# Weight sums in buffers of their own, output gates at eviction, a gate row folded into the output weights, four FFN tiles begun early

## The chip, the cores and the metric

The kernel runs on one core of a Trainium2 chip, as one launch. The time is that of the device in microseconds (us). Each kernel is timed several times and the median counts; one further execution is recorded by the hardware profiler.

## The reference

One block of a hybrid network on x of 1024 tokens by 1024 features, in float32. Cut to what matters here:

```
shift1, scale1, gate1, shift2, scale2, gate2 = split(silu(c) @ w_ada + b_ada, 6)
h = rms_norm(x) * (1 + scale1) + shift1
z, xbc, dt, qk, v, o, if_pre, gate_pre = split(h @ w_in)
y_ssd   = ssd_branch(z, xbc, dt, ...)                        # 2048 wide
y_mlstm = sigmoid(o) * (rms_norm(mlstm(qk, v, if_pre)) * norm_w)   # 4 heads of 512
g_ssd, g_mlstm = split(sigmoid(gate_pre), 2)
merged = g_ssd * (y_ssd @ w_branch_ssd) + g_mlstm * (y_mlstm @ w_branch_mlstm)
x = x + gate1 * (merged @ w_out)
h2 = rms_norm(x) * (1 + scale2) + shift2
gt, up = split(h2 @ w_ffn_in, 2)                             # 2816 wide each
x = x + gate2 * ((silu(gt) * up) @ w_ffn_out)
out = rms_norm(x) * final_norm_w
```

## The kernel before

Every float32 product is made as three matmuls of float32r operands: each operand is split into a rounded part and a rest (a cast on ScalarE, ACT, and a subtraction on VectorE, DVE; the helpers `split`, L123, and `split_pair`, L786), and high by high, high by low and low by high are summed in PSUM. TensorE (PE) thus works through some 12300 matmuls, most of them 128x128 by 128x512.

The program has these stages, in the order of the trace. First the modulation and the normalised, transposed x. Then the SSD branch: `conv_tile`, `z_gate` and `gate_tile` each call `gemm`, 48 matmuls against one 512 KB tile of `w_in`, and `ssd_pair` does the scan. Then the mLSTM, four heads: `ml_q`, `ml_k`, `ml_v` and `ml_scan`, with the gate tiles that are left set between the heads (`GP`, `GZ`). Then four projections by `strassen` (`ssd`, `ml`, `out`, and at the end `ffn`): each halves both operands in both directions and makes seven products instead of eight (p1 to p7), over sums and differences of quarters. Before `ffn` stands the FFN loop, 22 steps of the same kind over `w_ffn_in`: `head(j)` (24 matmuls, needs only the first half of the tokens) and five products (60 matmuls).

The weight side of `strassen` is prepared ahead by `prep_steps` and written to DRAM (`fac_*`): for each block of 128 rows all seven quarters and sums, A11, A12, A22, S1 to S4, split into two parts. `ssd`, `ml` and `out` are prepared between the tiles of the mLSTM stage; their raw rows take the ring `ld` and the split parts `fh`, `fl` the ring `cr`, both shared with the SSD scan and with `conv_tile`. `ffn` is prepared in the FFN loop, in the rings `raw`, `wh` and `wl` that also carry the weights of `head`. The writes go through the queue of GpSimd (POOL), nearly all loads through that of SyncE (SP).

`token_tile` loads 128x1024 tokens at the first use of a block; for `ml` it also loads the o gates into `og` (one buffer) and multiplies (L905, L906). The outputs of `out` are multiplied by gate1 (`g1`) after the product; scratch tiles `c`, `xr`, `sq`, `t2` share one ring of four buffers.

Nobody writes the order of the instructions on an engine by hand: a scheduler takes each instruction as early as its operands, buffers and engine allow, so that the size of a ring decides how early work can begin.

Of the kernel before, what the change touches and what calls it, by code (L numbers as in the profile page):

```python
# [15 lines left out]
P = 128  # L16
# [19 lines left out]
def hybrid_layer(ctx: ExitStack, tc: tile.TileContext, a: dict, out: bass.AP, dbg=None):  # L36
# [106 lines left out]
    FA = {"A11": 0, "A12": 1, "A22": 2, "S2": 3, "S3": 4, "S4": 5, "S1": 6}  # L143
    fac_d = {n: tc.dram_tile([kk, 7, P, 2, 512], F32, name=f"fac_{n}") for n, kk in (("ssd", 8), ("ml", 8), ("out", 4), ("ffn", 11))}

    def prep_steps(name, w_d, rawf, pairf):
        fd = fac_d[name]
        n = fd.shape[0]

        def put(r, kk, p0, cnt):  # L150
            wh, wl = pairf()
            m = cnt * 512
            A.copy(wh[:, 0:m], r[:, 0:m])  # L153
            V.tensor_tensor(wl[:, 0:m], r[:, 0:m], f(wh[:, 0:m]), SUB)  # L154
            for t, w in enumerate((wh, wl)):
                G.dma_start(fd[kk, p0:p0 + cnt, :, t, :].rearrange("f p n -> p f n"), f(w[:, 0:m]).rearrange("p (f n) -> p f n", n=512))

        for kk in range(n):
            r0, r1 = rawf(), rawf()
            Q.dma_start(r0, w_d[kk * P:(kk + 1) * P, :])  # L160
            Q.dma_start(r1, w_d[(kk + n) * P:(kk + n + 1) * P, :])
            put(r0, kk, FA["A11"], 1)
            yield
            put(r1, kk, FA["A12"], 2)
            a11, a21, a12, a22 = r0[:, 0:512], r0[:, 512:], r1[:, 0:512], r1[:, 512:]
            V.tensor_tensor(a22, a21, a22, ADD)
# [146 lines left out]
    def gemm(src, epi, w=None):  # L313
# [10 lines left out]
        next(later, None)  # L324

# [20 lines left out]
    def gate_tile(j):  # L346
# [7 lines left out]
        for _ in range(2):  # L354
            next(preps, None)
# [191 lines left out]
    def z_gate(r, Y=None):  # L547
# [14 lines left out]
        for _ in range(2):  # L562
            next(preps, None)
# [16 lines left out]
    def ml_v(h):  # L580

        vt = [xf("vt") for _ in range(4)]
        for u in range(2):
# [6 lines left out]
            for i in range(4):  # L590
# [14 lines left out]
                else:  # L605
# [9 lines left out]
    def ml_scan(h, q, k, v):  # L615
        C = ap.tile([P, 2, 514], F32, name="C")
        CH = CL = None
        for c in range(NCH):
# [79 lines left out]
            A.copy(yb[:, :, (c % 2) * L:(c % 2 + 1) * L], hps.rearrange("p (j l) -> p j l", l=L))  # L698
# [3 lines left out]
    gates = list(range(32))  # L702
# [16 lines left out]
    def phase_a_pair():  # L719
        return [ap.tile([P, 1024], F32R, name=n, tag="cr", bufs=NCR) for n in ("fh", "fl")]  # L720

    preps = chain(*(prep_steps(n, w, lambda: ld("fr"), phase_a_pair) for n, w in
                    (("ssd", a["w_branch_ssd"][0]), ("ml", a["w_branch_mlstm"][0]), ("out", a["w_out"][0]))))
# [67 lines left out]
    def strassen(name, b0, b1, order, sink, wq, nw, tq, nt, tmp, rows=False, odd=0):  # L791


        fd = fac_d[name]
        n = fd.shape[0]
        B0, B1 = {}, {}

        def t0(k):
            if k not in B0:
                B0[k] = b0(k)  # L800
            return B0[k]

        def t1(k):
            if k not in B1:
                B1[k] = b1(k)
            return B1[k]

        def tok(p, k):
            if p == 6:
                t2 = tmp()  # L810
                V.tensor_tensor(t2, t1(k)[:, H_], t0(k)[:, L_], SUB)
                m = split_pair(t2, tq, "tf", "tf", nt)
                V.tensor_tensor(t1(k)[:, L_], t1(k)[:, L_], t2, SUB)
                return m
            src = {1: lambda: t0(k)[:, L_], 2: lambda: t1(k)[:, L_], 3: lambda: t1(k)[:, H_], 4: lambda: t1(k)[:, L_],
                   5: lambda: t0(k)[:, L_], 7: lambda: t0(k)[:, H_]}[p]()
            m = split_pair(src, tq, "tf", "tf", nt)
            if p == 2:
# [31 lines left out]
    def sink_of(ut, tmp, final):  # L850

        U, U3 = {}, {}

        def sink(p, i, bank):
# [3 lines left out]
            elif p == 2:  # L858
                c = tmp()
                V.tensor_tensor(c, bank, U[i], ADD)  # L860
                final(0, 0, i, c)
# [24 lines left out]
    pb1, pb0 = pool(ctxD, "b1"), pool(ctxD, "b0")  # L886
# [364 lines left out]
```

## Time and profile before

| | |
|---|---|
| three runs | 2781.64, 2789.95, 2791.85 us; median 2789.95 |
| profiled execution | 2794.04 us, span of the trace 2792.3 us |
| PE busy | 2557.2 us (92%), mean granted clock 0.96 |
| DVE, ACT, POOL busy | 1795.5, 1105.2, 558.3 us |
| moved by DMA | 528.86 MB, mean 189 GB/s |

PE is busy nearly all the time, so the places where it is not are what to look for. A busy PE is not always at its full pace: the number of matmuls in a stretch tells more than the busy time.

### The profile page before, as it was taken

To read this page: it belongs to the slowest core of one execution; us is meant where nothing else is said; L and a number is where in the kernel's file an instruction comes from. 1 tells how busy PE (TensorE), PEld (TensorE's weight loads), DVE (VectorE), ACT (ScalarE), POOL (GpSimd) and SP (SyncE) were. 2 spreads that over 40 slices of the span, in tenths; PEclk is the share of its full clock that TensorE was granted. 3 is DMA by queue.
4 is the path that set the end of the run, shared out by engine and by line. 5 is a ranking of instruction groups with operands and counts; after the bars stand their busy time and mean duration, and the time that the engine had idled before them with its cause. 6 is when DMAs were issued, how large, how long until landed. Compare 5 with 4: busy or idle time off the path is not lost.

```text
span 2792.3 us, 34946 instructions
## 1 busy us (share of the span) xinstructions
PE 2557.2 (92%) x12907; PEld 2125.6 (76%) x12907; DVE 1795.5 (64%) x2768; ACT 1105.2 (40%) x1923; POOL 558.3 (20%) x627
## 2 busy tenths in 40 slices
PE   6999989999998999999999999797778999997898
PEld 4788878889876887988988778586557777775686
DVE  7577766895854566456555357554786878885436
ACT  5445544554442344345444423222253333332222
POOL 4000021110432013113133000000134444450001
PEclk9999999999999999999999999898889999998899
DMA  6333332345688458527654769565545666668566
GB/s 193 101 91 114 96 110 85 118 149 159 207 292 282 153 178 265 190 82 264 199 167 151 273 225 394 179 213 190 172 145 162 194 221 215 212 224 318 165 194 236
DMA packets 327826, 528.86 MB, mean 189 GB/s; under 512 B 21952, under 2 KB 208672, under 8 KB 327656
## 3 DMA queue, kind: packets, MB, share of 16 engines
q1 hardware_dynamic: 284968, 376.13, 42.7%
q0 software_dynamic: 42688, 150.49, 14.4%
q8 instruction: 102, 1.67, 0.2%
q14 instruction: 68, 0.56, 0.1%
HBM read 354.28 MB, written 172.27 MB: 189 GB/s over the span
## 4 chain that ended last, share of the span: by engine, by line
PE 59%; DMA 13%; DVE 12%; issue 8%; POOL 4%; ACT 3%; SPq 0%; POOLq 0%; DVEq 0%; ACTq 0%
PE mm L321 25%; PE n L838 10%; PE mm L601 7%; PE mm L838 5%; PE sc L838 4%; PE n L655 2%; DVE sw L786 1%; DMA raw<-in_w_ffn_out_dram 1%; DVE wl L154 1%; DMA fac_ffn<-wl 1%; DMA raw<-in_w_ffn_in_dram 1%; PE n L530 1%; DMA xr<-in_x_dram 1%; PE n L673 1%; PE n L1046 1%
## 5 line engine op out<-in xcount | busy, mean ns | idle before, releaser
L321 PE MATMUL mm<-hh,wh 128*128 128x512 f32 x1392 | 555.5, 399 | 31.9 <-ACT xf L333 20.7
L321 PE MATMUL mm<-hl,wh 128*128 128x512 f32 x1392 | 553.0, 397 | 0.0
L321 PE MATMUL mm<-hh,wl 128*128 128x512 f32 x1392 | 553.0, 397 | 0.0
L321 PEld LDWEIGHTS mm<-hh,wh 128*128 128x128 f32 x1392 | 265.1, 190 | 85.9 <-ACT xf L333 21.6
L321 PEld LDWEIGHTS mm<-hh,wl 128*128 128x128 f32 x1392 | 264.9, 190 | 52.9 <-issue 0.5
L321 PEld LDWEIGHTS mm<-hl,wh 128*128 128x128 f32 x1392 | 265.2, 191 | 51.7 <-issue 0.2
L123 DVE TENSOR_TENSOR wl<-raw,wh 128x1024 fp32r<-128x1024 f32 x126 | 158.6, 1259 | 153.2 <-PE mm L321 69.2
L122 ACT CAST wh<-raw 128x1024 fp32r<-128x1024 f32 x126 | 131.7, 1045 | 217.8 <-DMA raw<-in_w_in_dram 69.3
L786 DVE TENSOR_TENSOR tf<-bt,tf 128x512 fp32r<-128x512 f32 x162 | 110.6, 690 | 159.9 <-ACT tf L785 159.9
L785 ACT CAST tf<-bt 128x512 fp32r<-128x512 f32 x162 | 99.8, 621 | 255.0 <-PE sc L838 130.1
L154 DVE TENSOR_TENSOR fl<-fr,fh 128x512 fp32r<-128x512 f32 (+1 forms) x80 | 88.2, 1102 | 133.7 <-DMA fac_ssd<-fl 46.1
L341 DVE SCALAR_TENSOR_TENSOR xf<-cr,pk,xf 128x1023 f32<-128x1023 f32 (+2 forms) x120 | 160.2, 1336 | 17.8 <-ACT xf L333 16.7
L1046 PE MATMUL n<-t,sw 128*128 128x512 f32 x552 | 145.6, 409 | 25.9 <-ACT sw L785 7.7
L838 PE MATMUL n<-tf,wf 128*128 128x512 f32 x672 | 157.8, 393 | 9.7 <-ACT tf L785 7.8
L838 PEld LDWEIGHTS n<-tf,wf 128*128 128x128 f32 x672 | 127.3, 190 | 37.7 <-ACT tf L785 8.2
L838 PE MATMUL n<-wf,tf 128*128 128x512 f32 x540 | 129.5, 398 | 23.8 <-ACT tf L785 16.9
L1046 PEld LDWEIGHTS n<-t,sw 128*128 128x128 f32 x552 | 106.5, 196 | 56.0 <-ACT t L785 9.5
L838 PEld LDWEIGHTS n<-wf,tf 128*128 128x128 f32 x540 | 103.7, 193 | 47.0 <-ACT tf L785 17.4
L838 PE MATMUL mm<-wf,tf 128*128 128x512 f32 x360 | 97.9, 404 | 26.0 <-ACT tf L785 16.0
L153 ACT CAST fh<-fr 128x512 fp32r<-128x512 f32 (+1 forms) x80 | 75.4, 942 | 115.3 <-DMA fac_ml<-fh 28.8
L503 ACT ACTIVATE ab<-ab,gsum 128x128 f32<-128x128 f32 x256 | 78.4, 389 | 83.0 <-DMA ab<-acs_d 77.8
L559 POOL TENSOR_TENSOR Y<-Y,tz 128x512 f32<-128x512 f32 x14 | 31.0, 2236 | 389.0 <-DVE Y L540 222.5
(436 smaller groups left out, 5160.1 us busy)
## 6 DMA issues: line engine op xcount, KB each, us to landing
raw<-in_w_in_dram SPq DMA_DIRECT2D x104, 512.0 KB, 4.6
wf<-fac_ffn SPq DMA_DIRECT2D x77, 512.0 KB, 4.4
wf<-fac_ssd SPq DMA_DIRECT2D x56, 512.0 KB, 4.9
wf<-fac_ml SPq DMA_DIRECT2D x56, 512.0 KB, 3.7
rw<-in_w_ffn_in_dram SPq DMA_DIRECT2D x42, 512.0 KB, 4.5
raw<-in_w_ada_dram SPq DMA_DIRECT2D x40, 512.0 KB, 4.7
fac_ffn<-wh POOLq DMA_DIRECT2D x33, 512.0 KB, 4.2
fac_ffn<-wl POOLq DMA_DIRECT2D x33, 512.0 KB, 6.1
```

Of the source, the lines that this page charges most:

```text
L122: A.copy(wh, raw)
L123: V.tensor_tensor(wl, raw, f(wh), SUB)
L153: A.copy(wh[:, 0:m], r[:, 0:m])
L154: V.tensor_tensor(wl[:, 0:m], r[:, 0:m], f(wh[:, 0:m]), SUB)
L321: T.matmul(ps, lhsT=ww[:, k, :], rhs=xx[:, halves(hf)], start=n == 0, stop=n == 23)
L341: V.scalar_tensor_tensor(dst[:, sh:], cr[:, :S - sh], cw[:, 3 - sh, ti:ti + 1], dst[:, sh:], MUL, ADD)
L503: A.activation(ab[q][:, e, c], ab[q][:, e, c], AF.Relu, scale=-1.0, bias=acs_t[:, 4 * q + c, h0 + e:h0 + e + 1])
L601: T.matmul(ps[:, c], lhsT=hT[k][x_][:, sl], rhs=ws[k // 4][w_][:, k % 4], start=n == 0, stop=n == 23)
L785: A.copy(m[:, 0], t)
L786: V.tensor_tensor(m[:, 1], t, f(m[:, 0]), SUB)
L838: T.matmul(bk[i], lhsT=st[:, x, sl], rhs=mv[:, y], start=k == 0 and m == 0, stop=k == n - 1 and m == 2)
L1046: T.matmul(bank, lhsT=ww[:, k, :], rhs=b[k][:, r_], start=k == 0 and n == 0, stop=k == 3 and n == 2)
```

## The change

There are five parts. (1) `prep_steps` has buffers of its own: `pr` (two, for raw rows) and `pf` (one, for both split parts, written by one DMA). For `ssd`, `ml` and `ffn` it makes only S1 to S4; A11, A12 and A22 are loaded raw in `strassen` (`wt`) and split at use. `ffn` is prepared in the same chain, and none in the FFN loop; two steps follow each `gemm` and each part of `ml_v`. (2) The o gates are the first gate tiles (`ORD_G`), and `ml_scan` multiplies by them where it evicts its transposed output. (3) gate1 multiplies the rows of `w_out` in `prep_steps`, so the products of `out` need no multiplication. (4) Token blocks are loaded and scaled by half tiles of 128x512, and the scratch tiles have rings of their own. (5) Four heads of the FFN are begun ahead in place of two. The space for descriptors of GpSimd's DMAs is set to 2048 bytes a partition.

```diff
-    FA = {"A11": 0, "A12": 1, "A22": 2, "S2": 3, "S3": 4, "S4": 5, "S1": 6}
+    FA = {"S2": 0, "S3": 1, "S4": 2, "S1": 3, "A11": 4, "A12": 5, "A22": 6}
...
+        def pf():
+            return ap.tile([P, 2, 512], F32R, name="pf", bufs=1)
+
+        def put(r, kk, fa):
+            m = pf()
+            A.copy(m[:, 0], r)
+            V.tensor_tensor(m[:, 1], r, f(m[:, 0]), SUB)
+            G.dma_start(fd[kk, FA[fa]], f(m))
...
-            r0, r1 = rawf(), rawf()
+            r0, r1 = (ap.tile([P, 1024], F32, name="pr", bufs=2) for _ in range(2))
...
+            if gate is not None:
+                g = f(pf()).rearrange("p two n -> p (two n)")
+                Q.dma_start(g, gr_d[gate:gate + 1, :].broadcast_to([P, D]))
+                for r in (r0, r1):
+                    V.tensor_tensor(r, r, g, MUL)
+                yield
...
-            A.copy(yb[:, :, (c % 2) * L:(c % 2 + 1) * L], hps.rearrange("p (j l) -> p j l", l=L))
+            og = ap.tile([P, 4, L], F32, name="og", bufs=1)
+            Q.dma_start(og, tg_d[(16 + 4 * h) * P:(20 + 4 * h) * P, sl].rearrange("(j p) l -> p j l", p=P))
+            V.scalar_tensor_tensor(yb[:, :, (c % 2) * L:(c % 2 + 1) * L], og, 1.0, hps.rearrange("p (j l) -> p j l", l=L), ADD, MUL)
...
+    preps = chain(prep_steps("ssd"), prep_steps("ml"), prep_steps("out", 0), prep_steps("ffn"))
...
+        def weight(fa, k):
+            if FA[fa] < fd.shape[1]:
+                w = wq.tile([P, 2, 512], F32R, name="wf", tag="wf", bufs=nw)
+                Q.dma_start(f(w), fd[k, FA[fa]])
+                return w
+            t = wt_()
+            r0 = (k if fa == "A11" else k + n) * P
+            Q.dma_start(t, w_d[r0:r0 + P, halves(fa == "A22")])
+            return split_pair(t, wq, "wf", "wf", nw)
...
-        if g0 is not None:
-            og = sg.tile([P, 1024], F32, name="og", tag="og", bufs=1)
-            Q.dma_start(og, tg_d[(g0 + k) * P:(g0 + k + 1) * P, :])
-            V.scalar_tensor_tensor(t, og, 1.0, t, ADD, MUL)
...
+            Q.dma_start(t[:, halves(j)], src[r // 4][(r % 4) * P:(r % 4 + 1) * P, halves(j)])
+            A.activation(t[:, halves(j)], t[:, halves(j)], AF.Copy, scale=nw[:, r:r + 1])
...
+    def x_rows(tj, i, ci):
+        return rows_in(po, x_in, 4 * tj + i, ci, 6)
...
-    heads = [head(0), head(1)]
+    heads = [head(j) for j in range(NHEAD)]
...
-        if j % 2 == 0:
-            for _ in range(4):
-                next(preps, None)
```

On ACT, in the second group of the SSD scan, stood before:

```order
L332 COPY cr<-mm 128x512
L333 ACTIVATE xf<-mm,pk_108 128x512
L504 ACTIVATE ab<-ab 128x1024
L539 COPY Y<-n_1171 128x128
L503 ACTIVATE ab<-ab,gsum 128x128 x8
L332 COPY cr<-mm 128x512
L333 ACTIVATE xf<-mm,pk_108 128x512
L504 ACTIVATE ab<-ab 128x1024
L342 ACTIVATE cr<-xf 128x1024
```

and at the same place now (L158 is the cast of a weight sum, L345 the eviction of a convolution tile):

```order
L344 COPY cr<-mm 128x512
L345 ACTIVATE xf<-mm,pk_108 128x512
L513 ACTIVATE ab<-ab,gsum 128x128 x8
L514 ACTIVATE ab<-ab 128x1024
L158 CAST pf<-pr 128x512
L549 COPY Y<-n_1171 128x128
L513 ACTIVATE ab<-ab,gsum 128x128 x8
L344 COPY cr<-mm 128x512
L345 ACTIVATE xf<-mm,pk_108 128x512
L514 ACTIVATE ab<-ab 128x1024
L354 ACTIVATE cr<-xf 128x1024
L158 CAST pf<-pr 128x512
```

The casts of `pf` stand in the SSD stage, where no preparation was. Counting the evictions of convolution tiles (the first two come from another bank, the rest as `xf<-mm`), the 64 of `ssd` and `ml` have all come by the 48th; the 72 of `out` and `ffn` follow between the 56th eviction and the end of the third head's v, which comes after the 72nd.

On DVE, in the middle of the FFN loop, one step held before (L154, L166 to L169: preparation of `ffn`; L786: sums of `w_ffn_in`; the rest evicts products):

```order
L786 TENSOR_TENSOR sw<-s_18858,sw 128x512
L154 TENSOR_TENSOR wl<-raw,wh 128x1024
L1146 TENSOR_TENSOR u_18649<-mm,u_18649 128x512
L786 TENSOR_TENSOR sw<-rw,sw 128x512
L166 TENSOR_TENSOR raw<-raw 128x512
L1149 SCALAR_TENSOR_TENSOR u_18649<-tg,u_18649 128x512
L167 TENSOR_TENSOR raw<-raw 128x512
L1150 SCALAR_TENSOR_TENSOR u_18649<-u_18649,up 128x512
L168 TENSOR_TENSOR raw<-raw 128x512
L169 TENSOR_TENSOR raw<-raw 128x512
```

and the same step holds now (L125: split of a head's weights; L793: sums of `w_ffn_in`):

```order
L1126 TENSOR_TENSOR u_18629<-mm,u_18629 128x512
L793 TENSOR_TENSOR sw<-rw,sw 128x512
L1129 TENSOR_TENSOR u_19127<-sc,u_18629 128x512
L793 TENSOR_TENSOR sw<-rw,sw 128x512
L1132 TENSOR_TENSOR up<-n_19129,u_19127 128x512
L1133 TENSOR_TENSOR u_18629<-n_19129,u_18629 128x512
L793 TENSOR_TENSOR sw<-s_19089,sw 128x512
L1062 TENSOR_TENSOR v<-n_19055,u_19053 128x512
L125 TENSOR_TENSOR wl<-raw,wh 128x1024
```

The five instructions of the preparation are gone from it.

On SP's queue, in the middle of the `ssd` projection, the blocks of the `ml` projection are now loaded while the sums of `ssd` still stream in:

```order
L915 DMA bt<-y_d_79 128x512 x2
L813 DMA wf<-fac_ssd 128x1024
L915 DMA bt<-y_d_79 128x512 x2
L813 DMA wf<-fac_ssd 128x1024
L915 DMA bt<-y_d_79 128x512 x2
```

where before the loads of the o gates stood apart, each behind the last one's buffer, up into the loads of `fac_ml`:

```order
L905 DMA og<-tg_d 128x1024
L830 DMA wf<-fac_ml 128x1024 x2
L897 DMA tgl<-tg_d 128x512
L830 DMA wf<-fac_ml 128x1024
L905 DMA og<-tg_d 128x1024
L830 DMA wf<-fac_ml 128x1024 x2
```

The `og` loads have left this stage; the 32 of `ml_scan` are smaller and stand in the mLSTM stage.

## Rows read from the trace of the kernel before

**Rows 1.** Engines by stretch: busy us (instructions) of each, PE clock, DMA share, GB/s

```profile
0.00:100.00 100.00, 67.80 (x268) 47.71 (x269) 71.47 (x115) 52.96 (x115) 33.39 (x32) 0.93 0.55 161
100.00:640.00 540.00, 526.96 (x3062) 439.68 (x3061) 399.41 (x593) 274.10 (x546) 57.00 (x34) 0.99 0.35 111
740.00:920.00 180.00, 154.00 (x726) 128.84 (x726) 102.48 (x164) 66.48 (x102) 53.81 (x77) 0.91 0.79 268
1560.00:1620.00 60.00, 49.98 (x208) 39.41 (x207) 32.92 (x52) 22.15 (x32) 0.54 (x1) 0.96 0.79 276
1760.00:1800.00 40.00, 24.26 (x77) 17.55 (x78) 27.36 (x42) 10.02 (x14) 0.00 (x0) 0.79 0.48 162
1920.00:1960.00 40.00, 21.40 (x82) 16.71 (x81) 16.93 (x27) 8.93 (x19) 0.00 (x0) 0.74 0.43 140
2000.00:2120.00 120.00, 75.56 (x272) 55.26 (x271) 91.13 (x124) 55.30 (x96) 46.68 (x46) 0.76 0.43 137
2120.00:2500.00 380.00, 362.01 (x1546) 290.29 (x1545) 306.88 (x382) 132.23 (x200) 173.00 (x183) 0.99 0.66 213
2500.00:2580.00 80.00, 58.88 (x224) 46.32 (x223) 49.17 (x70) 16.36 (x26) 11.84 (x14) 0.83 0.81 304
2600.00:2640.00 40.00, 26.83 (x101) 20.58 (x100) 23.33 (x38) 8.28 (x17) 0.00 (x0) 0.79 0.44 135
2640.00:2760.00 120.00, 120.00 (x531) 99.38 (x530) 61.98 (x96) 31.12 (x56) 2.31 (x4) 1.00 0.69 221
```

**Rows 2.** Waits from 700 to 930 us: us in total, times, longest

```profile
PE mm L321 <- ACT xf L333: 16.4, 1, 16.4
...
ACT cr L332 <- DMA fac_ssd<-fh: 5.1, 1, 5.1
```

**Rows 3.** Chain that ended last, from 1740 to 1800 us: start, us, what

```profile
1753.56 4.45 DMA og<-tg_d
...
1758.03 1.24 DVE bt L906
```

**Rows 4.** Chain that ended last, from 1900 to 2125 us

```profile
1932.91 6.63 DMA xr<-in_x_dram
...
1984.63 4.78 DMA xr<-in_x_dram
...
2075.84 5.49 DMA fac_ffn<-wl
```

**Rows 5.** Chain that ended last, from 2120 to 2500 us

```profile
2191.61 10.32 DMA raw<-in_w_ffn_in_dram
```

**Rows 6.** Chain that ended last, from 2480 to 2660 us

```profile
2535.48 12.35 DMA bt<-act_d
```

**Rows 7.** Evictions of convolution tiles up to 560 and 640 us: ns, first and last start

```profile
L333 ACT ACTIVATE xf<-mm,pk x46: 769/783/799, 92.5 to 557.4; 128x512 f32<-128x512 f32 x46
L333 ACT ACTIVATE xf<-mm,pk x54: 769/783/799, 92.5 to 619.6; 128x512 f32<-128x512 f32 x54
```

**Rows 8.** ACT in order of time, first and eighth eviction of the third head's v

```profile
1163.50 0.59 ACT L602 COPY vt<-mm 128x512 f32<-128x512 f32 x1 [4.08 <-PE mm L601]
...
1204.14 0.59 ACT L602 COPY vt<-mm 128x512 f32<-128x512 f32 x1
```

**Rows 9.** Groups by line and shape: busy us, mean ns, idle before

```profile
L154 DVE TENSOR_TENSOR wl<-raw,wh 128x1024 fp32r<-128x1024 f32 x33 | 52.1, 1579 | 6.7 <-DMA fac_ffn<-wl 6.3 <-ACT wh L153 0.4
...
L154 DVE TENSOR_TENSOR fl<-fr,fh 128x512 fp32r<-128x512 f32 x20 | 14.2, 711 | 27.6 <-DMA fac_ssd<-fl 16.2 <-DMA fac_ml<-fl 9.1 <-DMA fac_out<-fl 0.9
...
L166 DVE TENSOR_TENSOR fr<-fr 128x512 f32<-128x512 f32 x20 | 13.7, 686 | 0.2
...
L153 ACT CAST fh<-fr 128x512 fp32r<-128x512 f32 x20 | 12.4, 622 | 31.2 <-DMA fac_ssd<-fh 12.2 <-DVE fl L154 6.6 <-DMA fac_ml<-fh 4.3
```

**Rows 10.** DMA issues by line: count, KB each, median us to landing

```profile
fac_ml<-fh POOLq DMA_DIRECT2D x24, 512.0 KB, 4.3
...
xr<-in_x_dram SPq DMA_DIRECT2D x16, 256.0 KB, 4.1
```

More of the change, by code (lines that the diff above doesn't have):

```diff
@@ L165, in prep_steps @@
             a11, a21, a12, a22 = r0[:, 0:512], r0[:, 512:], r1[:, 0:512], r1[:, 512:]
+            if fd.shape[1] == 7:
+                for fa, x in (("A11", a11), ("A12", a12), ("A22", a22)):
+                    put(x, kk, fa)
+                    yield
             V.tensor_tensor(a22, a21, a22, ADD)
@@ L324, in gemm @@
         next(later, None)
+        for _ in range(2):
+            next(preps, None)
     def conv_tile(col, cw, cb, ti, pre=None):
@@ L561, in z_gate @@
         gemm(w_in[:, OFF_Z + r * P:OFF_Z + (r + 1) * P], epi)
-        for _ in range(2):
-            next(preps, None)
         Q.dma_start(dst, Y)
@@ L604, in ml_v @@
                     next(later, None)
-                else:
+                for _ in range(2):
                     next(preps, None)
@@ L717, in hybrid_layer @@
     later = chain(mod_steps(2, mod_row, 0), mod_steps(3, mod_cols, 2), mod_steps(4, mod_cols, 3), mod_steps(5, mod_row, 1))
[L719 to L723, printed above, removed]
+    gp(2)
+    preps = chain(prep_steps("ssd"), prep_steps("ml"), prep_steps("out", 0), prep_steps("ffn"))
     q, k, v = ml_q(0), ml_k(0), ml_v(0)
@@ L789, in hybrid_layer, with strassen, blk @@
     L_, H_ = halves(0), halves(1)
-    def strassen(name, b0, b1, order, sink, wq, nw, tq, nt, tmp, rows=False, odd=0):
-        fd = fac_d[name]
+    def strassen(name, load, order, sink, wq, nw, tq, nt, wt_, t2_, rows=False, odd=0):
+        fd, w_d = fac_d[name], w_of[name]
         n = fd.shape[0]
[L796 to L806, printed above, removed]
+        B = {}
+        def blk(k, i, j):
+            if (k, i, j) not in B:
+                B[k, i, j] = load(k, i, j)[:, halves(j)]
+            return B[k, i, j]
+        def weight(fa, k):
[7 more added lines that the diff above has]
+            return split_pair(t, wq, "wf", "wf", nw)
@@ L1114, in rw_tile @@
         return e1[0].tile([P, 1024], F32, name="rw", tag="rw", bufs=3)
-    preps = prep_steps("ffn", a["w_ffn_out"][0], raw_tile, lambda: [wp.tile([P, 1024], F32R, name=n, bufs=b) for n, b in (("wh", NWH), ("wl", NWL))])
     for j in range(NFF):
@@ L1151, in hybrid_layer @@
                 G.dma_start(act_d[j * P:(j + 1) * P, H_], u1)
-        if j + 2 < NFF:
-            heads.append(head(j + 2))
-        if j % 2 == 0:
-            for _ in range(4):
-                next(preps, None)
+        if j + NHEAD < NFF:
+            heads.append(head(j + NHEAD))
     ctxF.close()
```

258 lines of the change are left out of this document (115 added, 143 removed).

## The prediction

> **What bounds the kernel now.** I read the table of engines by stretch first, because PE's 92% hides where it loses time. Where PE is undisturbed, 531 matmuls take 120 us, 0.226 us each; a stretch's length less its matmuls at that price is what PE loses there. The reader is to see in [rows 1] that the loss sits in a few places: 60 − 208 × 0.226 = 13.0 us at the start of the projections, 22.6 between `ssd` and `ml`, 21.5 inside `out`, 58.5 between `out` and the FFN loop (its 64 transposes are priced as full matmuls, so this is a lower bound), 30.6 over the FFN loop, 29.4 at the start of the last projection and 17.2 at its second turn. Together 193 us. The front half is nearly full: 527 of 540 us busy in the SSD stage, 26 us idle from 740 to 920. The chain of waits then says what PE waits for in each place, and the groups by shape give prices.
>
> **The FFN loop.** Preparing `ffn` leaves it. Its 33 wide subtractions alone took 52.1 us of DVE [rows 9], and with 11 narrow ones and 44 sums of at least 0.686 about 90 us, of DVE's 307 in 380 [rows 1]. The loop's waits follow from shared rings and an engine in order: a head's weights waited up to 10.32 us [rows 5]. Without it DVE falls to about 220 in 380 and `raw` serves the heads alone. POOL's own sums (173 us of 380) and the chains inside a step stay, so I don't take all 30.6: it falls to about 10, **−20**. Bounds: −8, if POOL's chains cause most of it, and −28.
>
> **Between `out` and the loop.** In the trace, loads of x rows stand in the chain at 1984.63, since their ring is shared with three kinds of scratch, and a write of `fac_ffn` holds it 5.49 us at 2075.84 [rows 4]. Both go: x rows have six buffers, g1's multiplications are gone, the preparation too. Two more heads, 48 matmuls or 10.8 us of PE work, can fill the gap, but they need 512 KB of weights each and two more DVE splits, where DVE is busy 91 of 120 us. The x1 write, which the in-place scaling still waits for, remains. From 58.5 to about 38, **−20** (−8 to −35).
>
> **The turns of the projections.** At 1753.56 the chain shows an `og` load of 4.45 us and its multiplication, 1.24 [rows 3]; one buffer, so four of these run in series while PE needs 12 × 0.226 = 2.7 us per block. That disappears, and the order of SP now has the `ml` blocks loaded during `ssd`. What comes in its place on ACT is per block of p1 one half-tile scaling and two casts, about 3 × 0.622 = 1.9 us [rows 9], and of p2 two and two, 2.5 us of PE's 2.7. That is close, so I leave 5 of 22.6. Inside `out`, p2's evictions wait for x rows, 6.63 us the first [rows 4]; with six buffers they come early: 21.5 to 6. At the start, p1 needs a 256 KB half and a 256 KB weight per block in place of 512 and 512: 13 to 6. Sum −17.6 − 15.5 − 7 = **−40** (−20 to −50).
>
> **The last projection.** Its blocks took 12.35 us at 2535.48 [rows 6], with DMA busy 0.81 [rows 1]: all token rows were loaded whole for p1. Half of those bytes now belong to p2, and p1's weights are half as many. The old h0 tiles come free two steps earlier. At the turn from p2 to p6 the x1 rows no longer share a ring. Of 29.4 + 17.2 I keep 21: **−25** (−10 to −36).
>
> Halving has its other side. A 256 KB load lands in 4.1 us, a 512 KB write in 4.3 [rows 10], so a half costs nearly the latency of a whole. [...] It becomes the third rival below.
>
> **The front half pays.** The order puts casts of `pf` into the SSD stage, not only into the mLSTM. There DVE is at 399 of 540 us; 64 subtractions at 0.711 and 64 sums at 0.686 [rows 9] are 89 us, some 78 of them after the first 100 us: 477 of 540, 88%. PE waits there for PSUM evictions by ACT, which has room (274 plus 64 × 0.622 = 40). I take 6 us (0 to 30). In the first 100 us DVE has 71, and is the engine that the start waits for; the order has there about 8 subtractions and 8 sums, 11 us, and two megabytes of loads ahead of modulation weights: 7 us (0 to 15). Together **+13**.
>
> **The mLSTM stage.** Before, PE lost 16.4 us at one eviction, because ACT waited for a `cr` buffer that a write of `fac_ssd` still read [rows 2]. That tie is gone. But each put now has one buffer: cast 0.622, subtraction 0.711, issue, and landing 4.3 [rows 10], about 6.4 with 0.7 for POOL's issue taken as the subtraction's size. The 64 of `ssd` and `ml` have up to 557 us, 8.5 each from 15 on; the 72 of `out` and `ffn` from 620 [rows 7] to about 1205, the last of eight evictions of the third head's v [rows 8], 8.1 each. So the chain keeps up on average. Beside those evictions of v the order has one put each, and they come (1204.14 − 1163.50) / 7 = 5.8 us apart [rows 8]: there ACT waits about 0.6 us each time, and two puts bunch elsewhere. Loading the o gates adds one 256 KB load per chunk, needed only at its end, and moves 32 evictions from ACT to DVE; nothing is queued behind them but the next chunk. Of the 26 us I take back **−12** (−26 to +15).
>
> [...]
>
> **The sum.** −20 − 20 − 40 − 25 + 13 − 12 = −104. From the profiled execution's 2794 that is **2690 us**. The runs' median stands 4 us below the profiled execution, which is within their spread, so I don't shift it. In the same way 0.5% (14 us) is about what a measurement can tell from no change.
>
> **The rivals.** *First, the one buffer paces everything* (the other side). If a put took c us, the chain needs 64c by the end of the SSD stage and 72c in the mLSTM. SP and ACT are in order: raw rows that wait for `pr`, and casts that wait for `pf`, hold back weight loads and evictions behind them, so PE falls behind with the chain. The lag is 64(c − 8.5) + 72(c − 8.1). The other terms give −92, so it breaks even at c = (92 + 544 + 583)/136 = 9.0 and is slower by 14 us at 9.1. At c = 8.6 it costs 6 + 36 = 42 and gives 2794 − 92 + 42 = 2744. For it speaks that an ACT at half load and a DVE at 88% delay each step, and that a smaller descriptor space might make POOL's issues wait; against it, that 8.1 is 27% above 6.4. Chance 0.10 for around 2744, 0.04 beyond 2808.
>
> *Second, DVE becomes the bound of the SSD stage.* If half of the 78 us shows, the +6 become +39: 2723. Against it, PE's evictions there are ACT's. Chance 0.10.
>
> *Third, the halves gain nothing at the starts*: 4.1 against 4.3 us [rows 10]. Then the first start and the last projection's first 80 us keep their loss: +7 and, of the 25, about 16 back: 2713. Chance 0.12.
>
> *Fourth, all goes its way*: every term at its better bound, −28 − 35 − 50 − 36 − 26 + 0 = −175, 2619; half-way between, about 2655. Chance 0.12.
>
> *Fifth, the waits only move*: PE's losses in FFN and `out` come back as waits on ACT and POOL; every gain at its lesser bound, −8 − 8 − 20 − 10 + 15 + 13 = −18: 2776. Chance 0.08.
>
> **How the numbers follow.** My forecast, 2690 with its own range 2660 to 2720, has 0.44. The second and third lie just above it, the first at 2744, the fourth below. 2645 to 2755 leaves out the slow end of the first, the fifth and half of the fourth's lower part: about 0.18. Faster by 14 us or more: all but the slow end and half of the fifth (2776 lies near the bound), 0.92; same 0.04; slower 0.04.
>
> **What would show it.** In the trace after: no `og`, `bt` or `xr` load of several us in the chain between 1550 and 2000; in the FFN loop some 90 matmuls per 20 us; DVE near 88% in the SSD stage with PE still above 95%; POOL's waits on the cast and the subtraction of `pf` short, and a spacing of about 8 us between its casts. I am wrong if casts of `pf` come at the pace of their DMA with PE idle beside them, if PE waits for DVE in the SSD stage, or if the FFN loop keeps its waits without the preparation.

## The result and the profile after

The changed kernel takes 2698.22 us (median of four runs, 2696.39 to 2699.43), the kernel before 2789.51 beside it: a ratio of 0.9677, with a 95% interval of 0.9657 to 0.9697. The forecast was 2690, with a range of 2645 to 2755. The profiled execution has a span of 2696.5 us.

The table of engines by stretch, of the changed kernel, in the columns of [rows 1]:

```profile
0.00:100.00 100.00, 63.20 (x251) 43.34 (x251) 74.35 (x119) 53.46 (x117) 36.47 (x38) 0.97 0.70 214
100.00:640.00 540.00, 498.08 (x2733) 409.24 (x2734) 433.94 (x645) 281.13 (x564) 82.84 (x91) 0.96 0.58 184
...
1590.00:1650.00 60.00, 58.71 (x260) 48.27 (x259) 47.67 (x77) 36.21 (x65) 1.08 (x2) 1.00 0.64 207
1790.00:1830.00 40.00, 35.34 (x143) 28.22 (x142) 26.70 (x44) 7.96 (x13) 0.00 (x0) 0.91 0.56 177
...
2000.00:2080.00 80.00, 60.30 (x229) 45.79 (x228) 62.31 (x86) 43.58 (x75) 25.38 (x21) 0.80 0.38 116
2080.00:2440.00 360.00, 360.00 (x1575) 295.76 (x1575) 232.49 (x313) 102.07 (x162) 127.49 (x117) 1.00 0.34 103
2440.00:2520.00 80.00, 65.53 (x281) 53.61 (x280) 57.54 (x91) 31.38 (x55) 3.76 (x6) 0.91 0.73 263
```

The back half is now nearly full: 1575 matmuls in the 360 us of the FFN loop are 0.229 us each. The front half is not. From 100 to 640 us PE is busy 498 us where it was 527 [rows 1]: 28.9 us more of idle, at a lower granted clock (0.96 against 0.99), with DVE busier. So the front has to be read as closely as the back, although the total is close to the forecast. The groups of the convolution, gate and q/k matmuls by line (count, ns, first and last start) date the end of the front half, before and after:

```profile
L321 PE MATMUL mm<-hh,wl x1392: 387/389/632, 76.3 to 1560.3; 128*128 128x512 f32 x199
```

```profile
L331 PE MATMUL mm<-hh,wl x1392: 387/389/796, 84.1 to 1597.3; 128*128 128x512 f32 x199
```

The last of them starts 37 us later than before. The kernel loses 37 us up to there and wins 133 after it.

To compare stages whose work has moved, I price every matmul of a trace by the spacing that its shape has where PE runs undisturbed: 0.226 us for 512 columns, 0.120 for 256, 0.119 for 258, 0.109 for 128 (0.058 with 64 stationary columns). What a stage lasts beyond the prices of the matmuls that start in it is PE's loss there. The boundaries are: 100 and 640 us; the last matmul of the rows above; the last of the third projection; the last of the FFN loop's first step; the last of the loop; the end. All in us:

| stage | before | after | change | forecast |
|---|---|---|---|---|
| startup, 0 to 100 | 52.0 | 55.9 | +3.9 | +7 |
| SSD, 100 to 640 | 36.7 | 80.6 | +43.9 | +6 |
| mLSTM, to 1560.3 and 1597.3 | 56.1 | 45.3 | −10.8 | −12 |
| first three projections, to 2000.8 and 1990.2 | 60.7 | 13.2 | −47.5 | −40 |
| gap to the FFN loop, to 2101.4 and 2075.3 | 63.6 | 37.3 | −26.3 | −20 |
| FFN loop, to 2529.2 and 2458.8 | 40.2 | 6.7 | −33.5 | −20 |
| last projection, to the end | 54.1 | 28.6 | −25.5 | −25 |
| sum | 363.4 | 267.5 | −95.8 | −104 |

The sum is the difference of the two spans. The total came out 8 us from the forecast because two errors nearly cancel: the first three rows are 36 us worse than forecast, the other four 28 us better.

The waits of PE from 100 to 640 us in the changed kernel (us in total, times, longest) show whom it waits for now:

```profile
PE mm L331 <- ACT xf L345: 7.1, 4, 4.8
PE sc L485 <- DVE xf L355: 5.2, 2, 5.1
...
PE n L527 <- DVE xe L524: 3.1, 1, 3.1
...
PE n L544 <- DVE st L534: 2.4, 2, 1.6
```

No single wait carries the loss. All the waits that the view lists add up to 43 us, in 21 waits; before the change they were 13 us, in 6. They are short ones at the scan's own steps, on evictions by ACT and on the scan's operands from DVE. None names a put. The longest, of PE and then DVE's order ahead of it, shows how a put can stand in the way:

```profile
490.67 2.05 PE L485 MATMUL sc<-xf 128*128 128x128 f32 x8 [5.05 <-DVE xf L355]
```

```profile
483.23 1.77 DVE L159 TENSOR_TENSOR pf<-pr,pf 128x512 fp32r<-128x512 f32 x1
...
488.33 2.29 DVE L355 SCALAR_TENSOR_TENSOR xf<-cr,xf 128x1024 f32<-128x1024 f32 x1
```

DVE works without a break from 479.8 us to the end of that L355; a put's subtraction of 1.77 us (L159) is one of the operations ahead of it.

The chain that ended last (start, us, what), at the turn from `ssd` to `ml` and at the start of the last projection:

```profile
1793.62 0.70 DVE c L863
...
1794.35 0.69 DVE c L939
1795.04 0.64 DVE c L863
1795.67 0.60 DVE am L940
...
2458.28 7.42 DMA wt<-in_w_ffn_out_dram
2465.72 1.22 ACT wf L792 x2
...
2468.24 4.71 DMA bt<-act_d
```

At the turn the gate loads of [rows 3] are gone. What is left there is DVE, which evicts the sums of the product that ends. At the start of the last projection the first block of tokens takes 4.71 us where it took 12.35 [rows 6], behind a first raw weight of 7.42 us and its split.

### The profile page after: what moved, and what is told of

It reads as the page before. It is cut to its first block, busy times and chain, and to the rows that moved or that the text cites. A ratio compares the mean times of both kernels' runs of the same rounds, so it can differ in the third digit from the quotient of the medians.

```text
span 2696.5 us, 35048 instructions
## 1 busy us (share of the span) xinstructions
PE 2538.0 (94%) x12907; PEld 2119.6 (79%) x12907; DVE 1779.0 (66%) x2861; ACT 1103.0 (41%) x2012; POOL 457.5 (17%) x515
## 3 DMA queue, kind: packets, MB, share of 16 engines
q1 hardware_dynamic: 307768, 356.48, 43.2%
q0 software_dynamic: 30528, 108.02, 10.5%
## 4 chain that ended last, share of the span: by engine, by line
PE 60%; issue 15%; DVE 9%; DMA 8%; ACT 4%; POOL 3%; SPq 0%; POOLq 0%; DVEq 0%; ACTq 0%
PE mm L331 16%; PE n L846 9%; PE n L1045 8%; PE mm L846 5%; PE sc L846 5%; PE mm L609 5%; PE mm L1045 4%; PE sc L1045 4%; DMA ab<-acs_d 2%; PE n L663 1%; ACT ab L513 1%; DVE wl L125 1%; PE n L681 1%; DMA bt<-y_d 1%; DMA pr<-in_w_branch_ssd_dram 1%
## 5 line engine op out<-in xcount | busy, mean ns | idle before, releaser
L125 DVE TENSOR_TENSOR wl<-raw,wh 128x1024 fp32r<-128x1024 f32 x126 | 162.0, 1286 | 124.0 <-PE mm L609 40.5
L158 ACT CAST pf<-pr 128x512 fp32r<-128x512 f32 x136 | 84.1, 618 | 261.1 <-DMA fac_ffn<-pf 66.9
L159 DVE TENSOR_TENSOR pf<-pr,pf 128x512 fp32r<-128x512 f32 x136 | 95.8, 705 | 128.8 <-ACT pf L158 128.3
L793 DVE TENSOR_TENSOR tf<-bt,tf 128x512 fp32r<-128x512 f32 x162 | 109.9, 686 | 98.2 <-ACT tf L792 98.2
L792 ACT CAST sw<-rw 128x512 fp32r<-128x512 f32 x84 | 51.5, 619 | 118.9 <-POOL rw L1075 51.9
```

The lines of the kernel that those rows point to most:

```text
L125: V.tensor_tensor(wl, raw, f(wh), SUB)
L158: A.copy(m[:, 0], r)
L159: V.tensor_tensor(m[:, 1], r, f(m[:, 0]), SUB)
L792: A.copy(m[:, 0], t)
L793: V.tensor_tensor(m[:, 1], t, f(m[:, 0]), SUB)
```

## The experiments

Each kernel is the changed one with a small edit. This is PE's loss by stage, as in the table above; the stages' ends move with each kernel. Each row comes from one trace. Between kernels that leave a stage alone the loss moves by up to 4 us, in the mLSTM stage by up to 7, so a difference of 5 or 6 us is little more than that.

| kernel | 0–100 | SSD | mLSTM | projections | gap | loop | last | time, ratio to before (95%) |
|---|---|---|---|---|---|---|---|---|
| changed kernel | 55.9 | 80.6 | 45.3 | 13.2 | 37.3 | 6.7 | 28.6 | 2698.2, 0.9677 (0.9657–0.9697) |
| e1_late8 | 53.1 | 55.7 | 71.0 | 13.2 | 37.6 | 5.6 | 29.2 | 2696.3, 0.9668 (0.9654–0.9683) |
| e2_late16 | 52.9 | 37.2 | 73.8 | 49.2 | 37.8 | 5.4 | 29.5 | 2719.3, 0.9757 (0.9740–0.9774) |
| e3_gsums | 53.8 | 77.6 | 67.8 | 13.0 | 37.4 | 6.7 | 28.7 | 2714.4, 0.9728 (0.9712–0.9745) |
| e4_inplace | 58.6 | 74.6 | 54.1 | 13.0 | 37.8 | 6.8 | 28.4 | 2704.9, 0.9698 (0.9684–0.9713) |
| e5_heads2 | 55.9 | 82.1 | 42.8 | 10.0 | 36.2 | 6.0 | 32.0 | 2697.0, 0.9683 (0.9667–0.9699) |
| e6_ogback | 55.9 | 80.3 | 51.4 | 14.0 | 36.7 | 6.6 | 28.9 | 2704.0, 0.9699 (0.9676–0.9722) |
| e7_whole | 55.9 | 79.6 | 48.4 | 9.7 | 37.3 | 6.7 | 34.1 | 2701.1, 0.9692 (0.9678–0.9707) |
| e8_rings | 55.9 | 84.1 | 38.6 | 25.7 | 43.1 | 6.4 | 28.0 | 2714.4, 0.9743 (0.9727–0.9758) |
| e9_ffnloop | 55.9 | 81.8 | 28.7 | 12.6 | 44.8 | 31.0 | 28.6 | 2714.0, 0.9732 (0.9705–0.9759) |
| e10_nosums | 55.2 | 65.4 | 51.2 | 11.7 | 37.0 | 6.7 | 28.6 | 2683.1, 0.9625 (0.9600–0.9650) |
| e11_late14in | 52.2 | 43.3 | 55.8 | 12.8 | 37.5 | 5.6 | 29.0 | 2667.3, 0.9569 (0.9545–0.9592) |
| e12_ogwhole | 55.9 | 84.5 | 53.4 | 15.8 | 37.1 | 6.6 | 28.6 | 2712.3, 0.9721 (0.9682–0.9760) |

### The loss in the SSD stage

**e1_late8 and e2_late16** move the start of the puts by a data dependency.

```diff
         V.scalar_tensor_tensor(Y, xs, dskip[:, r:r + 1], Y, MUL, ADD)
+        if r == 7:                       # 15 in e2_late16
+            V.tensor_copy(mk, Y[:, 0:1])
...
+            if name == "ssd" and kk == 0:
+                for r in (r0, r1):
+                    V.tensor_copy(r[:, 0:1], mk)
             Q.dma_start(r0, w_d[kk * P:(kk + 1) * P, :])
```

> Only the start of the weight sums is moved: the first raw rows wait for the eighth of the sixteen SSD pairs. In the changed kernel TensorE lost about 74 us between 100 and 640 us, against 36 before. Theory A (each put's cast, subtraction and share of the sums stands in front of the scan's own work on VectorE and ScalarE): about half of the puts leave the SSD stage, half of the 38 us come back, and the startup's 8 us too: about 2698 - 19 - 8 = 2671; the 136 puts at the 7.3 us they took in the mLSTM stage need 990 us and still end before the projections. Theory B (the chain on its one buffer sets the pace of the stage): the chain starts later and ends later, and nothing is won: 2690 to 2705. Theory C (the loss comes from something else in the change, such as the order of the gate tiles): 2698 with the SSD stage unchanged.

> The same with the first raw rows waiting for the sixteenth SSD pair, so that no put stands in the SSD stage. Theory A: the whole 38 us and the startup's 8 come back in the front, but 136 puts at 7.3 us from about 610 us on end near 1600, so that the end of the mLSTM stage waits for the chain or the puts slow it: about 2665 to 2690. Theory B: the chain paces the mLSTM stage instead, and the projections start later than in the changed kernel, whose last convolution matmul ended at 1597: 2700 to 2730. Theory C: the SSD stage still loses about 74 us.

A put is the cast, the subtraction and the write of one quarter or sum in `prep_steps`; the raw loads and the sums move with the puts here. Without puts in the SSD stage its loss is 37.2 us, as before the change (36.7). So the whole 43.9 us come from the puts and Theory C falls. But neither kernel is faster. With the start at the eighth pair, 37 of the 64 puts of `ssd` and `ml` move into the mLSTM stage. The SSD stage gives back 24.9 us and the mLSTM stage loses 25.7 more: with the one buffer a put costs about 0.7 us in either stage. Theory A was right on the place and wrong on the gain. The time lies in Theory B's span for another reason than B's: the last cast of a put starts at 1449 us, well ahead of the projections. With the start at the sixteenth it starts at 1613 us, after the mLSTM stage's own work. The casts and scalings of the first projection stand behind it in ACT's order, and PE waits for them. The longest wait of PE near 1600 us in that kernel, and the chain that ended last:

```profile
PE mm L853 <- ACT tf L799: 36.2, 1, 36.2
```

```profile
1610.31 2.89 DMA fac_ffn<-pf
1613.28 0.62 ACT pf L158
1614.41 0.62 ACT bt L923
```

**e4_inplace** asks whether the one buffer and the landing of its writes is what hurts.

```diff
-            m = pf()
-            A.copy(m[:, 0], r)
-            V.tensor_tensor(m[:, 1], r, f(m[:, 0]), SUB)
-            G.dma_start(fd[kk, FA[fa]], f(m))
+            m = ap.tile([P, 512], F32R, name="pf", bufs=2)
+            A.copy(m, r)
+            V.tensor_tensor(r.bitcast(F32R), r, f(m), SUB)
+            G.dma_start(fd[kk, FA[fa], :, 0], f(m))
+            G.dma_start(fd[kk, FA[fa], :, 1], r)
```

> The low part of a put is written in place over its raw rows, so that the same memory gives two buffers for the high part; each put is two DMAs of 256 KB in place of one of 512. VectorE and ScalarE do the same instructions. Theory A (instruction time): SSD stage unchanged, 2695 to 2700. Theory E (ScalarE, in order, waits for the landing of the last put: 53 us in the SSD stage, and holds the evictions behind it): these waits go, and 20 to 30 us of the 38 come back: 2670 to 2680.

In this kernel the sums for `out` are made from rows in which A11, A12 and A22 have already given way to their low parts, so its products differ from the reference's; the work is the same. The issues of the puts' writes, by tile (ns, first and last), of the changed kernel, and those of the first 64 puts of this one:

```profile
L160 POOL DMA_DIRECT2D fac_ffn<-pf x44: 532/540/579, 955.7 to 1252.6; - x44
L160 POOL DMA_DIRECT2D fac_ssd<-pf x32: 533/533/771, 44.6 to 322.6; - x32
L160 POOL DMA_DIRECT2D fac_ml<-pf x32: 531/533/597, 340.6 to 605.5; - x32
L160 POOL DMA_DIRECT2D fac_out<-pf x28: 533/540/616, 740.2 to 945.5; - x28
```

```profile
L160 POOL DMA_DIRECT2D fac_ssd<-pf x32: 539/539/773, 41.0 to 232.4; - x32
L160 POOL DMA_DIRECT2D fac_ml<-pf x32: 539/539/580, 248.6 to 436.0; - x32
```

The chain runs through in (436.0 − 41.0)/63 = 6.3 us a put where it took 8.9. ACT's waits for the landing of a put fall from 52.6 us to 2.3 in the SSD stage. Still that stage loses 74.6 us against 80.6, and the whole is 7 us slower. So the wait on the buffer is at most 6 us of the price (Theory E falls), and the chain does not pace the stage. The mLSTM stage loses 8.8 us more, and the time misses Theory A's span for it; why is not shown.

**e3_gsums** moves the sums to GpSimd.

```diff
-            V.tensor_tensor(a22, a21, a22, ADD)
+            G.tensor_tensor(a22, a21, a22, ADD)
...
```

> The four sums and differences of each block row of weights go from VectorE to GpSimd, all else as in the changed kernel. Theory A with VectorE's time as the cost: about 43 us of 84 leave VectorE in the SSD stage, and 10 to 20 us come back: 2680 to 2688. Theory D (GpSimd's own sums, which took about 1.8 us for 128x512 in this stage, slow VectorE beside them and the chain behind them): no gain or a loss, 2698 to 2715.

In the SSD stage 3 us come back, within what it moves by anyway, and the mLSTM stage loses 22.5 us more. DVE has fewer instructions, but longer ones. Groups by shape from 100 to 640 us (busy us, mean ns), of the changed kernel and of this one:

```profile
L159 DVE TENSOR_TENSOR pf<-pr,pf 128x512 fp32r<-128x512 f32 x58 | 41.0, 706 | 33.9 <-ACT pf L158 33.8
...
L355 DVE SCALAR_TENSOR_TENSOR xf<-cr,xf 128x1024 f32<-128x1024 f32 x24 | 33.5, 1395 | 9.3 <-ACT cr L354 9.1
```

```profile
L159 DVE TENSOR_TENSOR pf<-pr,pf 128x512 fp32r<-128x512 f32 x58 | 46.9, 808 | 51.3 <-ACT pf L158 51.2
...
L355 DVE SCALAR_TENSOR_TENSOR xf<-cr,xf 128x1024 f32<-128x1024 f32 x24 | 37.1, 1546 | 9.7 <-ACT cr L354 9.7
```

The sums that leave DVE in this stretch took 43.2 us, but DVE's busy time falls only from 433.9 us to 411.6. Theory D holds: about half of what GpSimd takes over comes back on DVE, at least in part in longer operations (L159 0.81 us in place of 0.71, L355 1.55 in place of 1.40).

**e10_nosums** leaves the four sums out.

```diff
-            V.tensor_tensor(a22, a21, a22, ADD)
-            V.tensor_tensor(a21, a11, a21, SUB)
-            V.tensor_tensor(a11, a22, a11, SUB)
-            V.tensor_tensor(a12, a12, a11, SUB)
```

> The four sums and differences of each block row are left out (the quarters themselves are split and written in their places, so the products of the weights are not the reference's); all casts, subtractions and transfers stay. Theory A with VectorE's time as the price: 43 of the 84 us that the puts cost VectorE between 100 and 640 us go, and about half of the 45 us that TensorE loses more there than before: 2698 - 20 = 2678 or lower. Theory F (the price is the place of the casts on ScalarE, or the issues and transfers, and not VectorE's time): 2693 to 2700.

The SSD stage loses 65.4 us, 15.2 less, and the time falls by about 15. By stretch, from 100 to 640 us:

```profile
100.00:640.00 540.00, 506.04 (x2857) 418.56 (x2857) 396.62 (x608) 287.05 (x577) 83.66 (x90) 0.97 0.59 188
```

DVE is at 397 us, as before (399 [rows 1]), and yet PE is busy 506 us and not 527. So the sums on DVE are part of the price, about a third of the 43.9 us. The time lies between those of the two theories, and each has a part. The other two thirds lie with what is left of the puts: the casts, the subtractions that wait for them, the issues and transfers. I did not separate these. Nor did I separate DVE's time from the shorter chain: without the sums the puts of `ml` end at 520 us in place of 605.

**e11_late14in** joins the two (the cut of its diff is against e4's `put`): the start waits for the fourteenth pair, and the low part is written in place, except for A11, A12 and A22 of `out`, which take a second buffer.

```diff
-            V.tensor_tensor(r.bitcast(F32R), r, f(m), SUB)
+            lo = r.bitcast(F32R) if fa[0] == "S" else ap.tile([P, 512], F32R, name="pf", bufs=2)
+            V.tensor_tensor(lo, r, f(m), SUB)
...
+        if r == 13:
+            V.tensor_copy(mk, Y[:, 0:1])
```

> The two experiments on the puts together: the raw rows wait for the fourteenth SSD pair, and the low part is written in place (except for A11, A12 and A22 of the third projection, which are needed again), so that the chain runs faster. The start alone gave 45 us back in the SSD stage and lost 52 at the end of the mLSTM stage, to a chain that ended at 1613; in place, 72 puts took 5.6 us each in the mLSTM stage. If 136 of them keep to 6.3 us from 560 on, they end near 1420, and a put costs TensorE about 0.3 us in the mLSTM stage against 0.7 in the SSD stage: 2675 to 2690. If a put costs the same wherever it stands, as with the start at the eighth pair: 2695 to 2705.

This is the fastest kernel, 2667.3 us, 31 below the changed kernel and 8 below the span that was expected. Engines by stretch, and the casts of its puts by tile:

```profile
100.00:640.00 540.00, 521.63 (x2954) 431.37 (x2953) 393.40 (x590) 270.54 (x544) 67.41 (x50) 0.99 0.39 122
640.00:1560.00 920.00, 890.65 (x5142) 779.19 (x5142) 571.79 (x1081) 385.51 (x680) 259.58 (x395) 0.99 0.65 214
```

```profile
L159 ACT CAST pf<-pr x136: 602/620/641, 593.7 to 1359.2; 128x512 fp32r<-128x512 f32 x136
```

All 136 puts run within 766 us, 5.7 each, nearly all in the mLSTM stage, and the last comes some 200 us before the projections start. The stage loses 55.8 us against 45.3 with 72 of them, 10.5 more. In the SSD stage the 64 others had cost 43.9. A late start alone gained nothing, at the eighth pair or at the sixteenth, and neither did the faster chain alone (e4). Why the 64 puts cost so little here is not shown: with the one buffer those moved by e1 cost 0.7 us each in the same stage, and e4's 72 in place cost no less there.

### The gains in the back half

**e9_ffnloop** prepares `ffn` in the loop again, in the rings of the heads' weights, S1 to S4 only.

```diff
-    preps = chain(prep_steps("ssd"), prep_steps("ml"), prep_steps("out", 0), prep_steps("ffn"))
+    preps = chain(prep_steps("ssd"), prep_steps("ml"), prep_steps("out", 0))
...
+    fpreps = prep_steps("ffn", late=True)     # raw_tile() and "wh" for pr and pf
     for j in range(NFF):
         u1, v = heads.pop(0)
+        if j % 2 == 0:
+            for _ in range(5):
+                next(fpreps, None)
```

> The preparation of the last projection's weights goes back into the FFN loop, in the rings of the heads' weights as before, with only S1 to S4 made; 44 puts leave the mLSTM stage. TensorE lost 30.6 us in that loop before and about 4 after. Theory A (it was this work on VectorE and in these rings that stalled the loop): some 20 to 26 us come back in the loop, and the mLSTM stage wins 44 puts at about 0.3 us each: 2698 + 23 - 13 = 2708. Theory B (the loop was relieved by the other parts): the loop stays at about 4, and the mLSTM stage's gain remains: 2685 to 2690.

```profile
2080.00:2440.00 360.00, 346.04 (x1483) 279.02 (x1482) 279.57 (x372) 114.91 (x191) 135.42 (x141) 0.99 0.54 175
```

In the same stretch the loop does 1483 matmuls where the changed kernel does 1575. It loses 31.0 us against 6.7, and the gap ahead of it 7.5 more. The mLSTM stage wins 16.6, about 0.38 us for each of the 44 puts. So Theory A holds: this preparation brings back 24 of the 33.5 us. The kernel before made all seven parts of a block, 77 in place of 44, so its own preparation may have cost more than these 24.

**e8_rings** puts x rows, squares and differences of `out` in one ring of four, and in `ffn` the rows and the squares (its differences keep their buffer).

```diff
-        A.activation(pl.tile([P, 512], F32, name="sq", tag="sq", bufs=1), ...
+        A.activation(pl.tile([P, 512], F32, name="sq", tag="xr", bufs=4), ...
...
-        return rows_in(po, x_in, 4 * tj + i, ci, 6)
+        return rows_in(po, x_in, 4 * tj + i, ci, 4)
...
-             lambda: po.tile([P, 512], F32, name="t2", tag="t2", bufs=2), rows=True)
+             lambda: po.tile([P, 512], F32, name="t2", tag="xr", bufs=4), rows=True)
```

> In the third and the last projection the x rows, the squares and the differences share one ring of four buffers again, in place of rings of their own of six, one and two. Theory A (x rows come late because of the shared ring, 6.63 us the first): 10 to 15 us come back inside the third projection and up to 10 in the last one: 2708 to 2723. Theory B (the gate multiplications that are gone were what held the ring): 2695 to 2703.

The projections lose 12.5 us more, the gap 5.8, the last projection nothing. Theory A holds for `out`, in size too, and not for the last projection. The loads of x rows are back in the chain that ended last:

```profile
1942.16 6.76 DMA xr<-in_x_dram
...
1993.93 4.29 DMA xr<-in_x_dram
```

**e5_heads2** has two heads ahead.

```diff
-NHEAD = 4
+NHEAD = 2
```

> Two FFN heads ahead in place of four, all else as in the changed kernel. TensorE lost 66 us between 2000 and 2120 us before and 33 in the same gap after. Theory A (the two more heads are 48 matmuls, 10.8 us of work that fills the gap): the gap loses about 11 us more, 2698 + 11 = 2709. Theory B (the gap is set by the chain through the x1 rows and their transposes, and the heads' 512 KB loads and splits stand in its way): no more is lost, 2693 to 2700.

The gap loses 36.2 us against 37.3, and the time is the same. So Theory A falls, and the time is Theory B's: the two more heads bring nothing. What sets the gap this run doesn't show.

**e6_ogback and e12_ogwhole** multiply by the o gates when the y blocks are loaded; e12 does it with whole tiles and one gate buffer, and loads whole tokens in `ssd` and `ml`.

```diff
-            V.scalar_tensor_tensor(yb[...], og, 1.0, hps.rearrange("p (j l) -> p j l", l=L), ADD, MUL)
+            A.copy(yb[...], hps.rearrange("p (j l) -> p j l", l=L))
...
+            if g0 is not None:
+                og = ogt()
+                Q.dma_start(og, tg_d[(g0 + r) * P:(g0 + r + 1) * P, halves(j)])
+                V.scalar_tensor_tensor(t[:, halves(j)], og, 1.0, t[:, halves(j)], ADD, MUL)
             A.activation(t[:, halves(j)], t[:, halves(j)], AF.Copy, scale=nw[:, r:r + 1])
```

> The o gates go back to the loading of the y blocks for the second projection, by half tiles with two buffers; the scan's eviction is a plain copy again. Theory A (each block's gate load of 4 us and its multiplication stand in series ahead of the projection): some 10 to 18 of the 22.6 us come back between the first and the second projection: 2708 to 2716. Theory B (with half tiles and two buffers the loads are early enough and hidden): 2695 to 2700.

> The o gates at the loading of the y blocks again, now with whole tiles of 128x1024 and one gate buffer, as before. Halves with two buffers lost about 4 us more between the first and the second projection, whole tiles without gates none. Theory A (one gate buffer and whole tiles in series make the wait): 10 to 14 us come back there, and 7 in the front as with the halves: 2712 to 2720. Theory B (the blocks now load early, during the first projection, whatever their size): 2700 to 2706.

The chain of e12 shows the series of [rows 3] again:

```profile
1788.27 3.72 DMA og<-tg_d
...
1792.01 1.24 DVE bt L920
...
1793.26 3.57 DMA og<-tg_d
...
1796.86 1.24 DVE bt L920
```

But the projections lose only 0.8 us more with halves and 2.6 with whole tiles, not the 10 us or more of either Theory A. The time of e12 is Theory A's all the same, for what other stages lose, and that of e6 is neither theory's. Counted in stretches of 80 us, the turn alone (1760 to 1840 us) lost 22.8 before, 8.1 after and 13.6 in e12. So the gate series, with the whole tiles, was about 5.5 of the turn's 14.7 us. SSD and mLSTM together lose 5.8 us more in e6 and 12.0 in e12, which is about what these stages move by anyway; that ACT's copies in place of DVE's products cost time there is not shown. The runs of e12 spread from 2700.7 to 2717.3, so its size is uncertain.

**e7_whole** loads and scales whole token blocks at their first use, in `ssd`, `ml` and `ffn`.

```diff
-        t, r = acts[k, i], (k + 11 * i) * P
-        Q.dma_start(t[:, halves(j)], act_d[r:r + P, halves(j)])
+            Q.dma_start(acts[k, i], act_d[r:r + P, :])
```

> Token blocks are loaded and scaled whole (128x1024, 512 KB) at their first use, in the first two projections and in the last; the weights stay as in the changed kernel. Theory A (half the bytes ahead of p1 are what opens the starts): the last projection's start, which lost 16.7 us after and 29.4 before, loses 8 to 12 us more, the first one 2 to 4: 2708 to 2714. Theory B (a half costs nearly the latency of a whole, 4.1 against 4.3 us): 2695 to 2700.

The last projection loses 5.5 us more, the first three nothing. Of the two theories neither has the size: the halves count at the last start, at half of what A says, and not at the first. Theory B's premise, that a half costs nearly the latency of a whole, does not hold at that start. The loads of its blocks (count, KB, median us to landing), of the changed kernel and of this one:

```profile
bt<-act_d SPq DMA_DIRECT2D x44, 256.0 KB, 5.4
```

```profile
bt<-act_d SPq DMA_DIRECT2D x22, 512.0 KB, 10.2
```

## Why the forecast was right, and where it was not

That 2690 came within 8 us of the time is luck in part: the first three stages together came out 36 us worse than forecast and the other four 28 us better.

**The front half** is the step that failed: +6 for the SSD stage, with a bound of 30, from "PE waits there for PSUM evictions by ACT, which has room", against +43.9 measured. The sign of being wrong that I had named, PE waiting for DVE in the SSD stage, is in the waits. In size it is the second rival (+39, chance 0.10), but not in its cause: DVE is at 434 of 540 us, not at 477, as less of the scan fits into the stretch, and its sums are a third of the loss (e10). I counted engine time against engine room. The loss has two parts that a busy share doesn't show. PE's idle time grew by 28.9 us, in short waits for an eviction or a scan step; that these stand in line behind a put is seen in the example above and argued for the rest. The other 15 us are pace: the granted clock was 0.96 in place of 0.99. In slices of 1 us it was 0.50 in 41 of the 540, in 9 before, and 1.00 in 485, in 527 before. e1 and e2 show that the puts are the cause, e4 that their buffer is at most 6 us of it. The startup's 7 us were 3.9.

**The first rival** (one buffer paces everything) did not come about. The cycle was 8.9 us in the SSD stage and (1252.6 − 740.2)/71 = 7.2 for the 72 puts of the mLSTM stage, from the issue of the first to that of the last. I had worked out 6.4, and had 8.5 and 8.1 to spend. So in the SSD stage the chain did fall behind its room, but PE did not fall behind with it, as e4 shows. POOL's issues of the puts, which the rival had perhaps waiting, took 0.53 to 0.54 us at the median and 0.77 at the most. The mLSTM term, −12, was −10.8, which is again a difference of two: in e9 the stage is 16.6 us better without 44 of its puts, a cost of which the forecast had only ACT's 0.6 us at eight evictions.

**The FFN loop**, −20, was −33.5. The mechanism was right, and e9 gives 24 us of it back. The size was off for two reasons. The stretch of 380 us that I priced had 30.6 us of loss, and the whole loop had 40.2. And I left 10 us for GpSimd's own sums and the chains in a step, where 6.7 remained. The other 9 us are not assigned; the 33 parts that the kernel before made and e9 does not are untested.

**The gap**, −20, was −26.3. The step that two more heads can fill the gap is wrong (e5). The shared ring was about 5.8 us of it (e8) and the preparation 7.5 (e9). Half of the gain is not assigned.

**The projections**, −40, were −47.5. Inside `out`, 15.5 was forecast and nearly all of the 21.5 went (from 1830 to 1980 us the changed kernel does 664 matmuls, 0.226 us each). e8 gives back 12.5, so the ring is the larger part. At the turn to `ml`, 17.6 was forecast and 14.7 came, but the gate series named as its cause is 5.5 of it (e12). What brings the other 9, and the start's gain (13.0 us of loss before, 60 − 260 × 0.226 = 1.2 after, where 7 was forecast), stays open: e7 shows that it is not the halves of the tokens. The raw weights, the order of the loads and two more buffers were not tried alone.

**The last projection**, −25, was −25.5, but the halved token blocks, which the forecast named first, are 5.5 of it (e7). The third rival, that halves gain nothing, is thus nearly right on what they bring, wrong on the reason (they do land sooner, in 5.4 us where the wholes took 10.2) and wrong on the time, since other parts bring the gain. Which parts these are is not shown.

## What to carry to other kernels

Work that is moved into a stage where TensorE is nearly full can cost it time although the other engines seem to have room: here 43.9 us, with DVE at 80% and ACT at 52%. It can delay the short steps that PE waits for: PE's idle time grew by 28.9 us, and the granted clock was 0.96 in place of 0.99. So ask not for the engine's share but for what stands behind the new work in its order. Before a chain of side work is spread over a program, try where it starts and how fast it runs together: here both edits brought 31 us where neither alone brought any. A total that meets its forecast proves little, as one stage was off by 38 us here and others made up for it.

## What the hardware showed beside this

Some of DVE's operations took about twice as long beside GpSimd's, 2.32 us in place of 1.23 and 1.39 in place of 0.69. DVE and GpSimd in order of time, near 325 us in the changed kernel:

```profile
324.30 1.22 DVE L516 TENSOR_TENSOR ab<-ab,cbm 128x1024 f32<-128x1024 f32 x1
325.43 2.32 DVE L355 SCALAR_TENSOR_TENSOR xf<-cr,xf 128x1024 f32<-128x1024 f32 x1
327.67 0.46 DVE L534 SCALAR_TENSOR_TENSOR st<-st,ecb,n 128x64 f32<-128x64 f32 x2
328.06 1.39 DVE L177 TENSOR_TENSOR pr<-pr 128x512 f32<-128x512 f32 x1
```

```profile
324.52 4.38 POOL L569 TENSOR_TENSOR Y<-Y,tz 128x512 f32<-128x512 f32 x2 [1.43 <-DVE Y L550]
328.86 3.95 POOL L579 TENSOR_TENSOR sqacc<-sqacc,sq 128x512 f32<-128x512 f32 x2
```

While GpSimd's first two operations run, L355 takes 2.32 us; its median over the kernel is 1.23. A 128x512 sum (L177), with GpSimd at work from its start to its end, takes 1.39 in place of a median of 0.69. L516, which started just before GpSimd, keeps its 1.22 us, and the next small operation of L534, at 329.37 us, its 0.27. Why some grow longer and others don't is not shown.

PE's granted clock fell to 0.50 after idle time. In this stretch of 20 us of the changed kernel PE waited 2.5, 0.8 and 3.6 us for DVE, and the mean granted clock was 0.66:

```profile
140.00:160.00 20.00, 13.00 (x54) 10.35 (x54) 14.62 (x24) 13.68 (x33) 0.54 (x1) 0.66 0.67 203
```

In slices of 2 us the clock was 1.00 up to 146 us, which takes in the first wait, 0.50 from 146 to 158 and 1.00 again from 160. From 156.3 to 158.9 us the matmuls of 512 columns started 0.43 us apart, from 160.2 on 0.23. From 120 to 160 us PE loses 12.9 us by the prices above, of which those waits are 6.9: here the loss was 6.0 us longer than the waits themselves.
